# Strassen weight sums fetched two units ahead with other turns of the accumulators, and the mLSTM and SSD gates computed with tokens on the partitions

## The chip, the core and the metric

The kernel runs on one core of a Trainium2 chip. The metric is the device time of one execution in microseconds (us); each kernel is executed several times and the median counts. The engines named below are PE (matrix products; PEld is its weight load, which overlaps the products), DVE (vector), ACT (scalar), POOL (GpSimd) and SP, which issues DMAs. POOL and ACT issue DMAs as well. Each engine works through its own list of instructions in order.

## The reference

One layer of a streaming encoder in fp32 on 512 prompt tokens and 64 sample tokens, treated together as 576 columns. Cut to what matters here:

```python
h = x + 0.5 * swiglu(rmsnorm(x, norm_ffn1), w_ffn1_in, w_ffn1_out)     # 1024 -> 2*4096 -> 1024
h = h + mixer(rmsnorm(h, norm_mix))
h = h + 0.5 * swiglu(rmsnorm(h, norm_ffn2), w_ffn2_in, w_ffn2_out)
y = rmsnorm(h, final_norm)

def swiglu(x, w_in, w_out):
    a, b = split(x @ w_in, 2);  return (silu(a) * b) @ w_out

# mixer: one input projection feeds an SSD scan (16 heads), band attention (8 heads), an mLSTM (4 heads)
dt = softplus(dt_raw + ssd_dt_bias);  a = -exp(ssd_a_log)          # 16 heads
cum = cumsum(dt * a)                                               # within a chunk
ig = mi + gb[:4];  lf = log_sigmoid(mf + gb[4:])                   # 4 heads
b = cumsum(lf);  logd = b_t - b_s + ig_s;  m = running max(...)    # mLSTM gates and stabiliser
```

## The kernel before

**Products.** The three stages follow each other on one core: FFN 1 (0 to about 600 us of the span), the mixer (about 600 to 1410, its merge included) and FFN 2. Activations lie with features on partitions and the 576 tokens as columns. A product in fp32 is made of three matmuls of a faster type: each operand is split into a high and a low part (`split`, lines 271 to 274: a cast on ACT writes the tile `ph` of a weight or `TH` of an activation, a subtraction on DVE writes `pl` or `TL`), and high x high, high x low and low x high are added.

**Units.** Most of the work goes through `stream`, which multiplies by seven products instead of eight (Strassen's scheme in Winograd's form). A unit is a 1024 x 256 piece of a weight matrix, four blocks q0 to q3 of 512 x 128. Its seven weight operands are T_A11 = q0, T_A22 = q2, T_A21 = q3, and four sums: T_X1 = q0+q1, T_X2 = q1+q2, T_X3 = T_X1+q2, T_X4 = T_X3+q3. A product is 12 matmuls of 128 x 288. `fetch` loads the pair (q0, q1) into a tile of the ring `wx` with SP (line 444) and at once has POOL issue a DMA that adds (q1, q2) to it while it is being transferred (line 445); three more loads bring q0, q2, q3 into the ring `wr` (line 449). T_X3 and T_X4 are then added on POOL (line 455): in the FFNs in place, onto the tile of T_X1, so that the T_X3 sum waits until T_X1 has been split, and T_X4 until T_X3 has been.

**Order.** `stream` goes through the products by a list `order` in which products of unit n stand between those of unit n-1, has operands made AHEAD = 5 products before their use, and asks for the blocks of unit n and n+1 when it first makes an operand of unit n. Four of the seven products add into the accumulator of T_X1 (X1, X3, A22, X2, with a readout after each), two into that of T_X4 (X4, A21), and A11 has one by itself. In the FFNs each of the three has two PSUM banks, which alternate from unit to unit. The readouts are in `swiglu`: g (line 602, ACT), P (line 607, ACT), a (lines 610 and 614, DVE), and in `residual`: R (line 630, DVE). A scheduler that simulates the engines fixes the final order of instructions on each engine; what the program is written in is its starting point.

**Mixer.** Its heads run as generators (jobs) that are advanced by `tick` between the products. All of them share PSUM tiles of the tags `x` (one buffer), `v` (one) and `s` (two). The gates are a further generator, `gates`: 20 rows (16 SSD heads, 4 forget gates) lie on partitions 0 to 63 with the 576 tokens along the free axis, softplus is evaluated by a polynomial on DVE (lines 763 to 780), running sums and maxima by scans (lines 789, 794, 804), the rows are written to a scratch in DRAM (`scr_rows`) from which the heads load broadcast copies, and the whole is turned by five transposes into `TM`, with tokens on partitions (line 827).

Of the kernel before, what the change touches and what calls it, by code (L numbers as in the profile page):

```python
# [42 lines left out]
WBUFS = {"wr": 5, "wx": 3, "wy": 2, "ph": 6, "pl": 6}  # L43
# [16 lines left out]
C_AL = 133  # L60
C_M0 = 134
C_CS = 135
C_N = 183
# [15 lines left out]
class Hybrid:  # L79
    def __init__(self, ctx, tc, I, O):  # L80
        self.tc, self.nc, self.I, self.O = tc, tc.nc, I, O
        self.plan = []
# [58 lines left out]
    def hidden_tiles(self, name):  # L141

        self.hidden.close()
        self.hidden.enter_context(self.pools(name, yp=dict(side="right")))
        self.YH, self.YL = self.pair_of(self.yp, [128, 8, T], ("YH", "YL"))
# [36 lines left out]

    def sm(self):
        return self.small.tile([128, 8], F32, name="sm", tag="sm")

    def setup(self):
        nc, c = self.nc, self.const
        self.cst = c.tile([128, C_N], F32, name="cst")
        self.ones = c.tile([128, 128], F32, name="ones")
        nc.gpsimd.memset(self.ones, 1.0)  # L190
        self.mhalf = c.tile([128, 1], F32, name="mhalf")
        nc.gpsimd.memset(self.mhalf, -0.5)

        nc.scalar.activation(self.sm(), self.ones[:, 0:8], AF.Silu)
        warm = self.ps("x")
# [80 lines left out]
    def sumsq(self, x, k, h, acc, first=None):  # L276
# [5 lines left out]
        sq = self.small.tile([128, 320], F32, name="sq", tag="sq", bufs=2)  # L282
# [43 lines left out]
    def norm(self, x, g0, hi, lo):  # L326

        nc = self.nc
        with self.tc.high_priority(offset=1500):
            for h, (a, n) in enumerate(HALVES):  # L330
                sl = slice(a, a + n)
                acc = self.small.tile([128, 320], F32, name="na", tag="na", bufs=1)
# [7 lines left out]
    def norm_first(self, x, g0, hi, lo, pin):  # L340
# [4 lines left out]
        for h, (a, n) in enumerate(HALVES):  # L345
            sl = slice(a, a + n)
            sq = self.sqp.tile([128, 8, n], F32, name="sq0", tag=f"sq{h}")
# [16 lines left out]
    def norm_out(self, x, g0, out):  # L364

        nc = self.nc
        with self.tc.high_priority(offset=1500):
            for h in (1, 0):
                a, n = HALVES[h]
                sl = slice(a, a + n)  # L370
                acc = self.small.tile([128, 320], F32, name="na", tag="na", bufs=1)
                pt = self.ps("x")
                for k in range(8):
                    if h == 0 and k == 7:
                        sq = self.small.tile([128, 320], F32, name="sq", tag="sq", bufs=2)
# [60 lines left out]
    def fetch(self, desc):  # L436
# [8 lines left out]
        nc.gpsimd.dma_start(x12, src[:, 1:3, :], accum_op=ALU.add)  # L445
# [24 lines left out]
    def stream(self, seq, order, banks):  # L470
# [4 lines left out]
        raw, ops, st = {}, {}, {}  # L475
# [183 lines left out]
    def ffn(self, x, g0, win, wout, name, last=(0, 1)):  # L659
# [99 lines left out]
    def gates(self, pre):  # L759
        nc = self.nc  # L760
# [6 lines left out]
        nc.vector.reciprocal(d[S, :], d[S, :])
        nc.vector.tensor_tensor(d[S, :], u[S, :], d[S, :], op=ALU.mult)
        yield
        nc.vector.tensor_tensor(q[S, :], d[S, :], d[S, :], op=ALU.mult)  # L770
        nc.vector.tensor_scalar(p[S, :], q[S, :], 1.0 / 15, None, op0=ALU.mult)
        for m in (13, 11, 9, 7, 5, 3):
            nc.vector.scalar_tensor_tensor(p[S, :], p[S, :], 1.0 / m, q[S, :], op0=ALU.add, op1=ALU.mult)
            if m % 4 == 3:
                yield
        nc.vector.scalar_tensor_tensor(p[S, :], p[S, :], 1.0, d[S, :], op0=ALU.add, op1=ALU.mult)
        nc.vector.tensor_scalar(u[S, :], pre[S, :], 0.0, None, op0=ALU.max)
        yield
        nc.gpsimd.memset(RT[64:128, :], 0.0)
        nc.vector.scalar_tensor_tensor(RT[S, :], p[S, :], 2.0, u[S, :], op0=ALU.mult, op1=ALU.add)  # L780
        lf, b, g, M = u, d, p, q
        nc.vector.tensor_scalar(lf[0:4, :], RT[32:36, :], -1.0, None, op0=ALU.mult)
        yield
        na = self.small.tile([128, 8], F32, name="ga", tag="ga", bufs=1)
        self.tc.keep_in_program_order(nc.scalar.activation(na[0:16, 0:1], self.cst[0:16, C_AL:C_AL + 1], AF.Exp))
        nc.vector.tensor_scalar(na[0:16, 0:1], na[0:16, 0:1], -1.0, None, op0=ALU.mult)
        nc.vector.tensor_scalar(da[0:16, :], RT[0:16, :], na[0:16, 0:1], None, op0=ALU.mult)
        for a, n in CH:
            nc.vector.tensor_tensor_scan(RT[32:48, a:a + n], self.ones[0:16, :n], da[0:16, a:a + n], 0.0,
                                         op0=ALU.mult, op1=ALU.add)  # L790
        nc.sync.dma_start(self.scr[0:16, :], RT[32:48, :])
        yield
# [16 lines left out]
        nm, ei = lf, da  # L809
# [4 lines left out]
        nc.vector.tensor_scalar(nm[0:4, :], M[0:4, :], -1.0, None, op0=ALU.mult)  # L814
# [7 lines left out]
        nc.scalar.activation(RT[96:100, :], b[0:4, :], AF.Exp, scale=-1.0)  # L822
        for c, (a, n) in enumerate(CH):
            if c % 2 == 0:
                yield
            ps = self.ps("x")
            nc.tensor.transpose(ps[:n, 0:128], RT[:, a:a + n], self.ident)
            nc.vector.tensor_copy(self.TM[:n, c, :], ps[:n, 0:128])
# [530 lines left out]
    def run(self):  # L1359
        nc, tc = self.nc, self.tc  # L1360
        x = self.R1
        with self.ffn_phase("a"):
            xin = self.I["xT"].rearrange("(k p) t -> p k t", p=128)
            with self.pools("a0", sqp=None):
# [17 lines left out]
        with self.pools("m", acc=self.PS, psp=self.PS):  # L1382
# [3 lines left out]
            with self.pools("m", tp=None, gp=dict(side="right")):  # L1386
# [3 lines left out]
                nc.gpsimd.memset(self.TM[:, 4, :], 1.0)  # L1390
# [9 lines left out]
    def branches(self, x):  # L1400
# [3 lines left out]
        with self.pools("m0", xp=None, op=None):  # L1404
            self.XH, self.XL = self.pair_of(self.xp, [128, 8, T], ("XH", "XL"))
# [54 lines left out]
def pack(plans, inp):  # L1460
# [9 lines left out]
    gate[:, 32:36] = w["w_in"][:, O_MF:O_MF + 4]  # L1470
    gate[:, 64:68] = w["w_in"][:, O_MI:O_MI + 4]
# [64 lines left out]
```

## Time and profile before

| | us |
|---|---|
| median of 3 runs (1981.6 to 1982.52) | 1981.8 |
| profiled execution: its own time | 1983.52 |
| profiled execution: span of its instructions | 1981.8 |
| PE busy in it (96% of the span) | 1901.4 |
| PEld / DVE / ACT / POOL busy | 1824.5 / 1461.5 / 1083.3 / 673.0 |
| granted clock of PE, mean | 0.982 |

The span is the time from the first to the last instruction; 1.7 us of the execution lie around it. Busy time of PE includes the overlap of pipelined matmuls, so a PE that is busy throughout is not idle but not necessarily at its best rate; PEld, of which there is one load for each matmul, shows gaps a little earlier than PE. The times below are from the start of the span.

### The profile page before, as it was taken

The numbers are of one execution on the slowest core, as the hardware profiler recorded it, in microseconds if no ns is written. First come the engines' busy times: TensorE is split into PE (matmuls) and PEld (weight loads), VectorE is DVE, ScalarE is ACT, GpSimd is POOL, SyncE is SP. The second block draws the span as 40 slices with busy tenths as digits, with TensorE's granted clock in tenths as the row PEclk, the third lists the DMA queues.
The fourth block names the chain that finished last, engine by engine and source line by source line (L and its number), as shares of the span: only waits on it lengthen the run. The fifth ranks groups of instructions, "written<-read, shape, count | busy, mean of one in ns | idle before, by whom it ended". The sixth has DMA issues, their size and how long they took to land.

```text
span 1981.8 us, 37575 instructions
## 1 busy us (share of the span) xinstructions
PE 1901.4 (96%) x13889; PEld 1824.5 (92%) x13889; DVE 1461.5 (74%) x2727; ACT 1083.3 (55%) x2487; POOL 673.0 (34%) x662
## 2 busy tenths in 40 slices
PE   9999999999999889999989998899999999999998
PEld 8899999999999759978889897899999999999998
DVE  8987877877668958667676774665798787787765
ACT  4554554544545577677586874333555454454444
POOL 5343333333202215322443443351233333333311
PEclk9999999999999879999999998999999999999999
DMA  7267666666742535753656668652236666656631
GB/s 215 72 158 174 151 155 163 149 167 168 184 128 96 131 104 145 212 149 110 178 150 180 162 169 246 203 167 86 75 97 160 160 150 161 162 151 161 174 109 63
DMA packets 130079, 297.04 MB, mean 150 GB/s; under 512 B 14416, under 2 KB 26320, under 8 KB 129896
## 3 DMA queue, kind: packets, MB, share of 16 engines
q1 hardware_dynamic: 100648, 208.03, 33.0%
q0 software_dynamic: 19760, 72.10, 19.9%
q10 hardware_dynamic: 9488, 14.52, 2.4%
q8 instruction: 109, 1.79, 0.4%
q14 instruction: 74, 0.61, 0.1%
HBM read 274.04 MB, written 20.56 MB: 149 GB/s over the span
## 4 chain that ended last, share of the span: by engine, by line
PE 35%; DMA 8%; DVE 3%; ACT 3%; issue 2%; POOL 1%; ACTq 0%; DVEq 0%; POOLq 0%; SPq 0%
PE acc L591 21%; PE acc L244 12%; DMA wx<-in_sblk 6%; DMA R<-scr_rows 1%; DVE pl L273 1%; ACT ph L272 1%; DMA y<-ys 1%; ACT R L1188 1%; DVE TL L273 0%; PE ps_s L1206 0%; PE ps_v L1228 0%; PE ps_x L1235 0%; DVE P L639 0%; DVE g L639 0%; DMA ys<-g 0%
## 5 line engine op out<-in xcount | busy, mean ns | idle before, releaser
L591 PE MATMUL acc<-TH,ph 128*128 128x288 f32 x3220 | 959.0, 300 | 31.9 <-ACT g L602 10.4
L591 PE MATMUL acc<-TL,ph 128*128 128x288 f32 x3220 | 952.8, 297 | 0.1
L591 PE MATMUL acc<-TH,pl 128*128 128x288 f32 x3220 | 944.1, 297 | 6.6 <-DVE pl L273 6.1
L591 PEld LDWEIGHTS acc<-TH,ph 128*128 128x128 f32 x3220 | 605.6, 189 | 52.3 <-ACT g L602 13.4
L591 PEld LDWEIGHTS acc<-TH,pl 128*128 128x128 f32 x3220 | 604.6, 189 | 14.3 <-DVE pl L273 11.1
L591 PEld LDWEIGHTS acc<-TL,ph 128*128 128x128 f32 x3220 | 607.8, 189 | 2.5 <-issue 1.9
L273 DVE TENSOR_TENSOR pl<-wr,ph 128x512 fp32r<-128x512 f32 x471 | 404.2, 863 | 83.4 <-ACT ph L272 76.3
L272 ACT CAST ph<-wx 128x512 fp32r<-128x512 f32 x390 | 233.4, 619 | 334.4 <-POOL wx L455 154.3
L273 DVE TENSOR_TENSOR pl<-wx,ph 128x512 fp32r<-128x512 f32 x390 | 286.1, 745 | 169.0 <-ACT ph L272 165.2
L272 ACT CAST ph<-wr 128x512 fp32r<-128x512 f32 x471 | 286.1, 616 | 202.9 <-PE acc L244 99.9
L455 POOL TENSOR_TENSOR wx<-wx,wr 128x512 f32<-128x512 f32 x160 | 226.0, 1413 | 446.0 <-DVE pl L273 411.8
L244 PE MATMUL acc<-YH,ph 128*128 128x256 f32 (+1 forms) x768 | 227.1, 300 | 9.0 <-DVE y L1303 5.3
L244 PE MATMUL acc<-YL,ph 128*128 128x320 f32 (+1 forms) x768 | 228.8, 299 | 2.1 <-DVE YL L323 2.1
L244 PE MATMUL acc<-YH,pl 128*128 128x320 f32 (+1 forms) x768 | 226.8, 298 | 0.0
L445 POOL DMA_DIRECT2D wx<-in_sblk x115 | 101.6, 892 | 239.1 <-DMA wx<-in_sblk 84.1
L244 PEld LDWEIGHTS acc<-YH,ph 128*128 128x128 f32 x768 | 146.9, 193 | 10.4 <-DVE y L1303 5.5
L244 PEld LDWEIGHTS acc<-YL,ph 128*128 128x128 f32 x768 | 146.8, 192 | 3.2 <-DVE YL L323 2.6
L244 PEld LDWEIGHTS acc<-YH,pl 128*128 128x128 f32 x768 | 146.5, 192 | 0.0
L455 POOL TENSOR_TENSOR wy<-wx,wr 128x512 f32<-128x512 f32 x35 | 51.4, 1468 | 184.2 <-DMA wx<-in_sblk 73.6
L630 DVE SCALAR_TENSOR_TENSOR R<-acc,R 128x288 f32<-128x288 f32 x168 | 73.2, 449 | 0.6 <-PE acc L591 0.4
L272 ACT CAST TH<-g 128x288 fp32r<-128x288 f32 x120 | 51.2, 433 | 38.6 <-DVE g L639 19.7
L616 POOL TENSOR_TENSOR g<-g,P 128x288 f32<-128x288 f32 x56 | 56.6, 1010 | 43.9 <-ACT P L615 43.9
(296 smaller groups left out, 2414.5 us busy)
## 6 DMA issues: line engine op xcount, KB each, us to landing
wr<-in_sblk SPq DMA_DIRECT2D x345, 256.0 KB, 4.3
wx<-in_sblk SPq DMA_DIRECT2D x115, 512.0 KB, 3.9
wx<-in_sblk POOLq DMA_DIRECT2D x115, 512.0 KB, 7.0
wr<-in_wblk SPq DMA_DIRECT2D x126, 256.0 KB, 3.2
R<-scr_rows ACTq DMA_DIRECT2D x12, 576.0 KB, 5.8
gs<-g SPq DMA_DIRECT2D x24, 288.0 KB, 4.7
y<-gs POOLq DMA_DIRECT2D x24, 288.0 KB, 3.4
y<-ys POOLq DMA_DIRECT2D x16, 288.0 KB, 4.4
```

Source lines behind the costliest of these rows:

```text
L244: nc.tensor.matmul(ps[:, :n], wt[:, wsl], xx[:, k0 + k, a:a + n], start=(k == 0 and i == 0), stop=(k == nk - 1 and i == 2))
L272: self.nc.scalar.copy(hi, src)
L273: self.nc.vector.tensor_tensor(lo, src, hi.bitcast(F32), op=ALU.subtract)
L445: nc.gpsimd.dma_start(x12, src[:, 1:3, :], accum_op=ALU.add)
L455: add = lambda o, one, two: self.nc.gpsimd.tensor_tensor(o, one, two, op=ALU.add)
L591: self.nc.tensor.matmul(ps, wt[:, wsl], xx[:, kk, :], start=(start and kk == 0 and i == 0), stop=(kk == 3 and i == 2), skip_group_check=True)
L616: nc.gpsimd.tensor_tensor(s["g"][:, 1, :], s["g"][:, 1, :], a, op=ALU.mult)
L630: self.nc.vector.scalar_tensor_tensor(o, ps, scale, o, op0=ALU.mult, op1=ALU.add)
L1188: nc.scalar.activation(e[:n, a:a + n], e[:n, a:a + n], AF.Relu, scale=-1.0, bias=self.TM[:n, c, tc_:tc_ + 1])
```

## The change

1. **Fetching.** `fetch` is split. `fetch_sums` loads (q0, q1) two units ahead instead of one; POOL's adding DMA for unit n+2 is issued when T_X3 of unit n is made, thus no longer right behind the load. The loads of q0, q2, q3 stay one unit ahead. The ring `wx` has 4 tiles instead of 3; the room comes from the squares of the norms, which move from a pool that lives throughout into pools of the stages.
2. **Turns.** In the FFNs T_X2 of unit n-1 comes before T_X4 of unit n instead of after it, and the six PSUM banks are dealt as three for T_X1, one for A11, two for T_X4. The mixer's order and banks stay.
3. **Gates.** `gates` first transposes the 24 raw rows, so that tokens lie on partitions and 5 x 20 values along the free axis, evaluates softplus there, takes the cumulative sums with one product against the triangular mask, transposes back for the running maxima and writes `TM` directly. Its PSUM tiles are one of tag `x` four times, and one of tag `s` once.

The core of the diff:

```diff
-WBUFS = {"wr": 5, "wx": 3, "wy": 2, "ph": 6, "pl": 6}
+WBUFS = {"wr": 5, "wx": 4, "wy": 2, "ph": 6, "pl": 6}
...
-    def fetch(self, desc):
+    def fetch_sums(self, desc):
...
         x12 = self.ring("wx", shape=(128, 2, 512))
         nc.sync.dma_start(x12, src[:, 0:2, :])
-        nc.gpsimd.dma_start(x12, src[:, 1:3, :], accum_op=ALU.add)
-        raw = {"x12": x12}
+        return {"x12": x12, "src": src}, lambda: nc.gpsimd.dma_start(x12, src[:, 1:3, :], accum_op=ALU.add)
+
+    def fetch(self, raw):
         for q in (2, 3, 0) if self.mixer else (0, 2, 3):
             raw[q] = self.ring("wr")
-            nc.sync.dma_start(raw[q], src[:, q, :])
-        return raw
+            self.nc.sync.dma_start(raw[q], raw["src"][:, q, :])
...
         def make(n, t):
-            for m in (n, n + 1):
-                if m < len(seq) and m not in raw:
-                    raw[m] = self.fetch(seq[m][0])
+            for m in range(n, min(n + 3, len(seq))):
+                if m not in raw:
+                    raw[m], begin[m] = self.fetch_sums(seq[m][0])
+                if m in begin and (m < n + 2 or t == self.T_X3):
+                    begin.pop(m)()
+                if m < n + 2 and 0 not in raw[m]:
+                    self.fetch(raw[m])
             ops[n, t] = self.operand(raw[n], t)
...
-        order = ((0, self.T_X1), (1, self.T_A22), (0, self.T_A11), (1, self.T_A21), (0, self.T_X3), (0, self.T_X4),
-                 (1, self.T_X2))
-        self.stream(seq, order, lambda n: {t: 3 * (n % 2) + i for i, t in enumerate((self.T_X1, self.T_A11, self.T_X4))})
+        order = ((0, self.T_X1), (1, self.T_A22), (0, self.T_A11), (1, self.T_A21), (0, self.T_X3), (1, self.T_X2),
+                 (0, self.T_X4))
+        self.stream(seq, order, lambda n: {self.T_X1: n % 3, self.T_A11: 3, self.T_X4: 4 + n % 2})
...
     def gates(self, pre):
-        u, d, p, q, RT, da = (self.R1[:, i, :] for i in range(1, 7))
-        S = slice(0, 64)
-        nc.scalar.activation(u[S, :], pre[S, :], AF.Abs)
...
+        X, u, d, p, q = view(1, 24), view(2, 20), view(3, 20), view(4, 20), view(5, 20)
+        for c, (a, n) in enumerate(CH):
+            nc.tensor.transpose(ps[:n, c * 24:(c + 1) * 24], pre[0:24, a:a + n], self.ident[0:24, 0:24])
...
-            nc.vector.tensor_tensor_scan(RT[32:48, a:a + n], self.ones[0:16, :n], da[0:16, a:a + n], 0.0,
-                                         op0=ALU.mult, op1=ALU.add)
...
+        nc.tensor.matmul(ps[:, 0:100], self.mask, self.R1[:, 3, 0:100], start=True, stop=True)
+        nc.vector.tensor_copy(TM[:, :, 32:48], sums[:, :, 0:16])
...
+        for dst, r, m in ((b, 96, 4), (g, 64, 4), (RT, 32, 16)):
+            nc.scalar.copy(dst[0:m, 0:512], ps[r:r + m, :])
+            nc.scalar.copy(dst[0:m, 512:576], ps2[r:r + m, 0:64])
```

How it stands on the engines, at three places. First POOL in FFN 1, in a stretch of `swiglu` units; `wx<-in_sblk` is the adding DMA, `wx<-wx,wr` a T_X3 or T_X4 sum, `g<-g,P` a product of `swiglu`. Before:

```order
L445 DMA wx<-in_sblk 128x1024
L455 TENSOR_TENSOR wx<-wx,wr 128x512 x2
L616 TENSOR_TENSOR g<-g,P 128x288
L445 DMA wx<-in_sblk 128x1024
L455 TENSOR_TENSOR wx<-wx,wr 128x512 x2
```

and now:

```order
L451 DMA wx<-in_sblk 128x1024
L462 TENSOR_TENSOR wx<-wx,wr 128x512
L628 TENSOR_TENSOR g<-g,P 128x288
L462 TENSOR_TENSOR wx<-wx,wr 128x512
L451 DMA wx<-in_sblk 128x1024
```

The adding DMA stands between the two sums of a unit instead of ahead of or behind both, and serves the unit after next.

Second DVE at the start of the mixer's stream, where the gates begin; `R_60` is the tile that the gates work in, `pl` the low part of a weight, `g<-acc,uv` a readout of a product. Before:

```order
L767 RECIPROCAL R_60<-R_60 64x576
L273 TENSOR_TENSOR pl<-wy,ph 128x512
L273 TENSOR_TENSOR pl<-wx,ph 128x512
L517 SCALAR_TENSOR_TENSOR g<-acc,uv 128x288
L768 TENSOR_TENSOR R_60<-R_60 64x576
L517 SCALAR_TENSOR_TENSOR g<-acc,uv 128x288
```

and now:

```order
L279 TENSOR_TENSOR pl<-wr,ph 128x512
L791 RECIPROCAL R_60<-R_60 128x100
L529 SCALAR_TENSOR_TENSOR g<-acc,uv 128x288
L792 TENSOR_TENSOR R_60<-R_60 128x100
L529 SCALAR_TENSOR_TENSOR g<-acc,uv 128x288
L794 TENSOR_TENSOR R_60<-R_60 128x100
```

The same steps stand among the same neighbours, with 100 elements on a partition instead of 576.

Third PE later in the mixer, where for some time no product of `stream` (`acc`) stands in its list and two attention heads follow each other: `ps_x<-ident,P` turns probabilities, `ps_s<-g` makes scores, `ps_v<-Q,t` the weighted sums, `R_60` the gates' transposes, `ps_x<-ident,g` the next head's values. Before, from the last product on:

```order
L591 MATMUL acc<-TH_7247,pl 128x288
L827 MATMUL ps_x<-ident,R_60 128x128
L917 MATMUL ps_s<-g 128x384
L827 MATMUL ps_x<-ident,R_60 128x128
L903 MATMUL ps_x<-ident,P 128x128 x4
L903 MATMUL ps_x<-ident,P 64x128
L966 MATMUL ps_v<-Q,t 64x64 x8
L827 MATMUL ps_x<-ident,R_60 64x128
L966 MATMUL ps_v<-Q,t 64x64 x2
L917 MATMUL ps_s<-g 128x384
L858 MATMUL ps_x<-ident,g 128x128 x4
```

and now:

```order
L603 MATMUL acc<-TH_7252,pl 128x288
L931 MATMUL ps_x<-ident,P 128x128 x4
L983 MATMUL ps_v<-Q,t 64x128
L945 MATMUL ps_s<-g 128x256
L983 MATMUL ps_v<-Q,t 64x128 x7
L931 MATMUL ps_x<-ident,P 128x128 x4
L945 MATMUL ps_s<-g 128x384
L931 MATMUL ps_x<-ident,P 64x128
L994 MATMUL ps_v<-Q,t 64x64 x10
L886 MATMUL ps_x<-ident,g 128x128 x4
```

The gates' transposes have left this stretch, and the end of the first of the two heads has come into it: from the last product before it to the first behind it there are 58 instructions instead of 48. In the second half of the mixer's stream PE's list is the same in both kernels.

More of the change, by code (lines that the diff above doesn't have):

```diff
@@ L59 @@
 C_GB = 132
-C_AL = 133
+C_AL = 183
 C_M0 = 134
 C_CS = 135
-C_N = 183
+C_N = 203
 O_Z, O_X, O_B, O_C, O_DT = 0, 1024, 2048, 2560, 3072
@@ L143, in hidden_tiles @@
         self.hidden.close()
-        self.hidden.enter_context(self.pools(name, yp=dict(side="right")))
+        self.hidden.enter_context(self.pools(name, yp=dict(side="right"), qp=dict(side="right")))
+        self.sqp = self.qp, {"na": 1, "sq": 2}
         self.YH, self.YL = self.pair_of(self.yp, [128, 8, T], ("YH", "YL"))
@@ L181, in ps, with squares @@
         return self.psp.tile([128, 512], F32, name="ps_" + tag, tag=tag, bufs=self.pbufs[tag])
+    def squares(self, tag):
+        pool, bufs = self.sqp
+        if pool is self.op:
+            return self.op.tile([128, T], F32, name=bufs[tag], tag=bufs[tag], bufs=2)[:, :320]
+        return pool.tile([128, 320], F32, name=tag, tag=tag, bufs=bufs[tag])
     def sm(self):
@@ L281, in sumsq @@
             return
-        sq = self.small.tile([128, 320], F32, name="sq", tag="sq", bufs=2)
+        sq = self.squares("sq")
         nc.scalar.activation(sq[:, :n], x[:, k, a:a + n], AF.Square)
@@ L331, in norm @@
                 sl = slice(a, a + n)
-                acc = self.small.tile([128, 320], F32, name="na", tag="na", bufs=1)
+                acc = self.squares("na")
                 for k in range(8):
@@ L346, in norm_first @@
             sl = slice(a, a + n)
-            sq = self.sqp.tile([128, 8, n], F32, name="sq0", tag=f"sq{h}")
+            sq = self.s0.tile([128, 8, n], F32, name="sq0", tag=f"sq{h}")
             pt = self.ps("x")
@@ L370, in norm_out @@
                 sl = slice(a, a + n)
-                acc = self.small.tile([128, 320], F32, name="na", tag="na", bufs=1)
+                acc = self.squares("na")
                 pt = self.ps("x")
@@ L374, in norm_out @@
                     if h == 0 and k == 7:
-                        sq = self.small.tile([128, 320], F32, name="sq", tag="sq", bufs=2)
+                        sq = self.squares("sq")
                         nc.scalar.activation(sq[:, :n], x[:, k, sl], AF.Square)
@@ L771, in gates @@
-        nc.vector.tensor_scalar(p[S, :], q[S, :], 1.0 / 15, None, op0=ALU.mult)
-        for m in (13, 11, 9, 7, 5, 3):
[L773 to L777, printed above, removed]
-        yield
-        nc.gpsimd.memset(RT[64:128, :], 0.0)
@@ L796, in gates @@
-        nc.vector.tensor_copy(g[0:4, :], pre[64:68, :])
-        nc.vector.tensor_tensor(g[0:4, :], g[0:4, :], b[0:4, :], op=ALU.subtract)
-        nc.vector.tensor_copy(RT[64:68, :], g[0:4, :])
+        nc, TM = self.nc, self.TM
+        view = lambda i, w: self.R1[:, i, 0:5 * w].rearrange("p (c w) -> p c w", w=w)
+        X, u, d, p, q = view(1, 24), view(2, 20), view(3, 20), view(4, 20), view(5, 20)
+        nc.gpsimd.memset(X[64:128, 4, :], 0.0)
+        ps = self.ps("x")
+        for c, (a, n) in enumerate(CH):
+            nc.tensor.transpose(ps[:n, c * 24:(c + 1) * 24], pre[0:24, a:a + n], self.ident[0:24, 0:24])
@@ new lines, in gates @@
+        nc.vector.tensor_copy(X[:, 0:4, :], ps[:, 0:96].rearrange("p (c w) -> p c w", w=24))
+        nc.vector.tensor_copy(X[:64, 4, :], ps[:64, 96:120])
+        yield
+        S = X[:, :, 0:20]
+        nc.vector.tensor_scalar(X[:, :, 16:20], X[:, :, 16:20], -1.0, None, op0=ALU.mult)
+        nc.scalar.activation(u, S, AF.Abs)
+        nc.scalar.activation(u, u, AF.Exp, scale=-1.0)
+        nc.vector.tensor_scalar(d, u, 2.0, None, op0=ALU.add)
+        nc.vector.reciprocal(d, d)
+        nc.vector.tensor_tensor(d, u, d, op=ALU.mult)
@@ new lines, in gates @@
+        yield
+        nc.vector.tensor_tensor(q, d, d, op=ALU.mult)
+        nc.vector.tensor_scalar(p, q, 1.0 / 15, None, op0=ALU.mult)
+        for m in (13, 11, 9, 7, 5, 3):
+            nc.vector.scalar_tensor_tensor(p, p, 1.0 / m, q, op0=ALU.add, op1=ALU.mult)
+        nc.vector.scalar_tensor_tensor(p, p, 1.0, d, op0=ALU.add, op1=ALU.mult)
+        nc.vector.tensor_scalar(u, S, 0.0, None, op0=ALU.max)
+        sp = p
+        nc.vector.scalar_tensor_tensor(sp, p, 2.0, u, op0=ALU.mult, op1=ALU.add)
@@ new lines, in gates @@
+        na = self.R1[:, 5, 200:220]
+        self.tc.keep_in_program_order(nc.scalar.activation(na, self.cst[:, C_AL:C_AL + 20], AF.Exp))
+        da = d
+        nc.vector.scalar_tensor_tensor(da, sp, -1.0, na.unsqueeze(1).broadcast_to([128, 5, 20]),
+                                       op0=ALU.mult, op1=ALU.mult)
+        nc.vector.tensor_copy(TM[:, :, 0:16], sp[:, :, 0:16])
+        yield
+        ps = self.ps("x")
+        nc.tensor.matmul(ps[:, 0:100], self.mask, self.R1[:, 3, 0:100], start=True, stop=True)
@@ new lines, in gates @@
+        sums = ps[:, 0:100].rearrange("p (c w) -> p c w", w=20)
+        nc.vector.tensor_copy(TM[:, :, 32:48], sums[:, :, 0:16])
+        nc.vector.tensor_copy(TM[:, :, 96:100], sums[:, :, 16:20])
+        nc.vector.tensor_tensor(TM[:, :, 64:68], X[:, :, 20:24], TM[:, :, 96:100], op=ALU.subtract)
+        yield
+        RT, b, g, M, ei = (self.R1[:, i, :] for i in (6, 2, 3, 4, 5))
+        ps, ps2 = self.ps("x"), self.ps("s")
+        for c, (a, n) in enumerate(CH):
+            o = ps[:, a:a + n] if c < 4 else ps2[:, 0:n]
+            nc.tensor.transpose(o, TM[:n, c, :], self.ident[:n, :n])
@@ L813, in gates @@
         nc.sync.dma_start(self.scr[20:24, :], ei[0:4, :])
-        nc.vector.tensor_scalar(nm[0:4, :], M[0:4, :], -1.0, None, op0=ALU.mult)
+        nm = g
+        nc.scalar.activation(nm[0:4, :], M[0:4, :], AF.Copy, scale=-1.0)
         nc.sync.dma_start(self.scr[16:20, :], nm[0:4, :])
@@ L821, in gates @@
         nc.sync.dma_start(self.O["m"], mo[0:4, :])
-        nc.scalar.activation(RT[96:100, :], b[0:4, :], AF.Exp, scale=-1.0)
+        nc.scalar.activation(b[0:4, :], b[0:4, :], AF.Exp, scale=-1.0)
+        yield
+        ps = self.ps("x")
         for c, (a, n) in enumerate(CH):
[L824 to L828, printed above, removed]
+            nc.tensor.transpose(ps[:n, c * 4:c * 4 + 4], b[0:4, a:a + n], self.ident[0:4, 0:4])
+        nc.vector.tensor_copy(TM[:, 0:4, 96:100], ps[:, 0:16].rearrange("p (c w) -> p c w", w=4))
+        nc.vector.tensor_copy(TM[:64, 4, 96:100], ps[:64, 16:20])
     def rows(self, r0, n, step=0):
@@ L1363, in run @@
             xin = self.I["xT"].rearrange("(k p) t -> p k t", p=128)
-            with self.pools("a0", sqp=None):
+            with self.pools("a0", s0=None):
                 self.setup()
```

44 lines of the change are left out of this document (12 added, 32 removed).

## The prediction

> **What bounds the kernel now.** I read the page first, its line of engines:
>
> ```profile
> PE 1901.4 (96%) x13889; PEld 1824.5 (92%) x13889; DVE 1461.5 (74%) x2727; ACT 1083.3 (55%) x2487; POOL 673.0 (34%) x662
> ```
>
> PE is busy for 96%, so no more than the gaps of PE can be won unless its work shrinks, and the change removes none of it. Then I cut the span into stretches and looked for PEld's gaps, since there is one load for each matmul. Busy time of PE, PEld, DVE, ACT and POOL, the clock and the DMA share follow each other in these rows, two from the middle of each FFN's stream and one from near its end:
>
> ```profile
> 100.00:500.00 400.00, 390.89 (x2906) 386.24 (x2905) 307.66 (x544) 204.46 (x432) 147.41 (x128) 1.00 0.65 161
> 500.00:580.00 80.00, 80.00 (x611) 80.00 (x610) 53.16 (x100) 38.37 (x78) 12.36 (x12) 1.00 0.55 150
> 1490.00:1850.00 360.00, 350.79 (x2588) 344.40 (x2588) 276.61 (x488) 177.54 (x377) 130.32 (x113) 1.00 0.62 158
> 1850.00:1930.00 80.00, 80.00 (x604) 80.00 (x603) 56.85 (x89) 42.72 (x85) 22.13 (x20) 1.00 0.52 140
> ```
>
> Where nothing is late PEld is busy 80.00 of 80.00 us. In the two streams 400 - 386.24 = 13.8 and 360 - 344.40 = 15.6 us are missing: 29.4 us, all at full clock. That is what this change's first two parts can win. The waits of PEld name what ended them, FFN 1 first, then FFN 2 (us in total, times, longest):
>
> ```profile
> PEld acc L591 <- ACT g L602: 5.1, 4, 2.0
> PEld acc L591 <- DVE R L630: 4.1, 5, 1.2
> PEld acc L591 <- DVE pl L273: 2.4, 6, 1.0
> PEld acc L591 <- ACT P L607: 1.8, 4, 0.4
> ```
>
> ```profile
> PEld acc L591 <- ACT g L602: 8.0, 8, 2.2
> PEld acc L591 <- ACT P L607: 3.6, 7, 0.7
> PEld acc L591 <- DVE pl L273: 2.2, 9, 0.4
> PEld acc L591 <- DVE R L630: 0.9, 2, 0.5
> PEld acc L591 <- DVE g L618: 0.6, 1, 0.6
> ```
>
> PE is held by readouts of accumulators, not by weights. The timeline of ACT at one of the longest says why the readout was late; the last row is PE's:
>
> ```profile
> 376.98 0.62 ACT L272 CAST ph<-wx 128x512 fp32r<-128x512 f32 x1 [3.45 <-DMA wx<-in_sblk]
> 377.50 0.44 ACT L611 ACTIVATE P<-P 128x288 f32<-128x288 f32 x1
> 377.84 0.60 ACT L272 CAST ph<-wr 128x512 fp32r<-128x512 f32 x1
> 378.35 0.39 ACT L602 COPY g<-acc 128x288 f32<-128x288 f32 x1
> ```
>
> ```profile
> 378.79 0.40 PE L591 MATMUL acc<-TH,ph 128*128 128x288 f32 x1 [1.81 <-ACT g L602]
> ```
>
> ACT stood 3.45 us in front of a cast whose weight sum had not landed, and the copy that PE needed was three instructions behind it. Over the two streams ACT waits so often:
>
> ```profile
> ACT ph L272 <- DMA wx<-in_sblk: 47.4, 25, 3.7
> ```
>
> ```profile
> ACT ph L272 <- DMA wx<-in_sblk: 47.0, 24, 3.7
> ```
>
> Most of these waits are absorbed; those that are not are the g L602 and R L630 rows above.
>
> **The sums, two units ahead.** The path of a sum is SP's load, then POOL's adding DMA:
>
> ```profile
> wx<-in_sblk SPq DMA_DIRECT2D x115, 512.0 KB, 3.9
> wx<-in_sblk POOLq DMA_DIRECT2D x115, 512.0 KB, 7.0
> ```
>
> ```profile
> DMA to landing us min/median/max: 5.5/7.0/13.4
> ```
>
> ```profile
> 1850.00:1930.00 80.00, 68.01 (x509) 67.55 (x507) 1.00 0.52 140
> ```
>
> The first two rows are the load and the adding DMA from the page's list of issues, with their median time to landing; the third gives the spread of the adding one. The last row is line 591 alone: 68.01 / 509 = 0.134 us a matmul, so a product of 12 takes 1.60 us and a unit of 84 takes 11.2. Before, load and adding DMA need 3.9 + 7.0 = 10.9 us and are asked for one unit, 11.2 us, ahead of the cast: nothing is left for a queue, and the longest waits are 3.7 us. Now the load is asked for two units ahead (22.4 us). The adding DMA is issued four products later (6.4 us, over 3.9), so POOL no longer stands waiting for the load, and ten products, 16 us, before the cast, over the longest landing of 13.4. I take the g L602 and R L630 rows as gone: 5.1 + 4.1 + 8.0 + 0.9 = 18.1 us. Bytes and number of DMAs stay; the ring's fourth tile is released by the same unit n-2 as the third was, so SP's loads of q0, q2, q3, which stand behind the load of the pair, wait no longer than now.
>
> **The turns.** In the written order before, X1 of unit n+1 follows directly on X2 of unit n-1, which had its bank; the scheduler evades this by another order in which A22 comes closely behind X3, and P L607 is late. Now each readout has at least three other products, 4.8 us, before its accumulator is used again. Readouts take 0.39 us (row 378.35), so with a free queue this is enough: 1.8 + 3.6 + 0.6 = 6.0 us gone. The pl rows, 2.4 + 2.2 = 4.6 us, concern DVE's splitting and I let them stand. Sum of both parts: -24.1 us; bounds -29.4 (all gaps) and -12 (half, if DVE becomes late, below).
>
> **The gates.** Rows of DVE between 640 and 720 us (count, busy us, mean ns):
>
> ```profile
> L773 DVE SCALAR_TENSOR_TENSOR R<-R 64x576 f32<-64x576 f32 x6 | 5.0, 838 | 0.0
> L767 DVE RECIPROCAL R<-R 64x576 f32<-64x576 f32 x1 | 3.7, 3745 | 0.0
> L768 DVE TENSOR_TENSOR R<-R 64x576 f32<-64x576 f32 x1 | 1.5, 1477 | 0.0
> L780 DVE SCALAR_TENSOR_TENSOR R<-R 64x576 f32<-64x576 f32 x1 | 0.7, 741 | 0.0
> ...
> L1163 DVE TENSOR_TENSOR wd<-R,TM 128x4 f32<-128x4 f32 x2 | 0.3, 158 | 0.8 <-DMA R<-scr_rows 0.8
> ```
>
> From 4 to 576 elements an instruction grows from 158 to 741 ns, so 100 elements are an estimated 0.26 us (bounds 0.16 and 0.74) and the reciprocal 3.745 x 100/576 = 0.65. These four groups, 9 instructions and 10.9 us, become 8 x 0.26 + 0.65 = 2.7: DVE is relieved of 8 us there, and of some more by the scans that a product replaces. ACT gains six copies, three of them at most 0.6 us each. What it is worth stands in the stages and in PE's waits between 640 and 740 us:
>
> ```profile
> 640.00:710.00 70.00, 64.16 (x401) 53.77 (x399) 59.91 (x132) 43.96 (x109) 23.05 (x31) 0.93 0.55 151
> ...
> 709.00:734.50 25.50, 19.75 (x73) 9.09 (x72) 9.63 (x32) 15.64 (x52) 1.85 (x5) 0.60 0.29 66
> ```
>
> ```profile
> PEld acc L591 <- DVE g L517: 3.3, 2, 2.1
> ...
> PEld ps_x L903 <- ACT P L894: 3.5, 1, 3.5
> ```
>
> Up to 710 us DVE is busy 59.91 of 70 us, and PE's two groups of waits there, 6.8 us, hang on it; I take 5 of them as won. Against it stands the stretch without products behind it: 25.5 us at a clock of 0.60 for 48 of PE's instructions, 0.53 us each. There are 58 now, which costs 10 x 0.53 = 5.3 us. Together 0; bounds -9 (all waits won, the stretch unchanged, its clock better) and +8 (nothing won, three readouts later).
>
> **The rest of the mixer.** One stall there is of the kind above, ACT first, then PE:
>
> ```profile
> 952.69 0.62 ACT L272 CAST ph<-wx 128x512 fp32r<-128x512 f32 x1 [4.54 <-DMA wx<-in_sblk]
> ```
>
> ```profile
> 954.30 0.49 PE L1206 MATMUL ps_s<-t 128*128 128x128 f32 x2 [1.91 <-ACT st L1209]
> ```
>
> -1.9 us, bounds -4 and +4 since the order between 720 and 900 us shifts by a product or two.
>
> **The start.** One more adding DMA goes ahead of POOL's next work:
>
> ```profile
> 27.54 2.87 POOL L445 DMA_DIRECT2D wx<-in_sblk  x3
> 33.11 0.72 POOL L290 TENSOR_TENSOR sm<-sm,mhalf 128x2 f32<-128x2 f32 x1 [2.70 <-DVE sm L309]
> ```
>
> It takes about 1 us of the 2.70 that POOL waits anyway: 0; if that cover is gone, +1. The norms' squares have as many tiles as before: 0.
>
> **Sum.** -24.1 + 0 - 1.9 + 0 = -26.0 us. The profiled execution took 1983.5 us (span 1981.8 and 1.7 around it), the median of the runs shown is 1981.8, 0.1% less; 1957.5 for an execution like the profiled one, 1955.8 for the median. I forecast **1956 us**.
>
> **Rivals.** (A) DVE takes the place of ACT. PE then waits for pl and for readouts on DVE. For it: some splits of weights already run long in FFN 1 (x, min/median/max ns):
>
> ```profile
> L273 DVE TENSOR_TENSOR pl<-wx,ph x139: 673/685/1654, 99.4 to 499.6; 128x512 fp32r<-128x512 f32 x139
> L273 DVE TENSOR_TENSOR pl<-wr,ph x105: 673/684/1757, 101.7 to 494.8; 128x512 fp32r<-128x512 f32 x105
> ```
>
> The long ones lose 1.0 us each. If both POOL sums of each of the 36 units in that window cost DVE this much, that is at most 72 us on 307.66, 380 of 400: still under the window, but with no slack for bursts, and half the gain would go: 1981.8 - 12 = 1970. Against it: part of these losses is in the 307.66 already, and the number of sums does not change. The Trainium skill ("SBUF — State Buffer", section "Who interferes with whom") speaks for this rival: a vector instruction with two inputs in SBUF and a GpSimd instruction that reads SBUF shut each other out for a whole instruction. The maxima agree with it, and now X2's split stands between the two sums, where before DVE mostly waited. By the rule at its fullest the sum would be this rival's, by the medians mine.
>
> (B) The mixer wins too: with DVE free the first head ends earlier and the 25.5 us stretch shrinks by the 9 us above, with 3 to 4 more elsewhere: 1944. Against it: PE's list has more in that stretch, not less.
>
> (C) Slower. The new gates hold the only PSUM tile of tag x while ACT copies it six times, and the heads' turns wait for the same tile; the stretch without products grows. At 0.53 us an instruction it eats the 26 us from 49 more instructions, or from a length of 51.5 us, on; then 1986 and more. Against it: the list shows 10 more, not 49.
>
> (D) The change doesn't do what it says: sums land earlier, but ACT waits as long for POOL's sums (T_X3, T_X4) and PE for the same readouts: 1981.
>
> **Chances.** Forecast 0.62 (its own range 1946 to 1967), A 0.16, B 0.10, C 0.07, D 0.05. A change within 0.2%, 4 us, is about what a measurement of this kernel cannot tell from none. So faster 0.62 + 0.16 + 0.10 = 0.88, same 0.05, slower 0.07. The range takes in the forecast, most of B and of A: 1943 to 1974.
>
> **What would show it.** In the profile after, ACT's waits for the DMA of wx in the two windows fall from 94 us to below 10, PEld's gaps there from 29.4 to about 5, with pl as the first releaser; POOL's adding DMA waits for no load. DVE's busy time from 640 to 710 us falls by about 8; the stretch without products lasts about 31 us. Wrong would be: gaps of the old size under other names (A, D), or a stretch over 40 us at half clock (C).

## The result and the profile after

The changed kernel takes 1946.6 us (median of 4 runs, 1945.1 to 1949.5), the kernel before 1981.7: the ratio is 0.9825, its 95% interval 0.981 to 0.984. It is faster by 35 us; 26 were forecast. 1946.6 lies in the range, and nearer to rival B (1944) than to the forecast (1956). The profiled execution took 1949.5 us, its span is 1947.5. Its line of engines:

```profile
PE 1890.3 (97%) x13901; PEld 1824.7 (94%) x13901; DVE 1533.7 (79%) x2715; ACT 1099.2 (56%) x2494; POOL 669.9 (34%) x660
```

DVE is busy for 72 us more than before, although it has 12 instructions fewer and shorter gates. The stretches, with the columns of before (the last row is the new stretch without products in the mixer, now from 695.5 us on):

```profile
100.00:500.00 400.00, 397.72 (x2971) 395.82 (x2970) 361.26 (x551) 214.69 (x440) 151.42 (x132) 1.00 0.65 165
640.00:710.00 70.00, 65.22 (x406) 50.75 (x404) 43.62 (x122) 51.38 (x143) 17.04 (x21) 0.94 0.60 165
1490.00:1850.00 360.00, 357.94 (x2670) 355.59 (x2669) 317.85 (x492) 188.80 (x385) 135.83 (x117) 1.00 0.63 163
695.50:716.80 21.30, 20.07 (x90) 10.25 (x89) 8.82 (x27) 11.81 (x33) 1.92 (x4) 0.70 0.31 76
```

PEld's gaps in the two streams are 4.2 + 4.4 = 8.6 us instead of 29.4. What ended them, FFN 1 and then FFN 2:

```profile
PEld acc L603 <- ACT g L614: 2.3, 4, 0.9
PEld acc L603 <- DVE P L622: 1.5, 3, 0.5
PEld acc L603 <- ACT P L619: 0.3, 1, 0.3
```

```profile
PEld acc L603 <- ACT P L619: 1.7, 4, 0.5
PEld acc L603 <- DVE P L622: 1.7, 4, 0.5
PEld acc L603 <- ACT g L614: 1.0, 2, 0.5
```

ACT's waits for the DMA of `wx` (94 us in the two streams before) are gone; these are its two longest groups now, in FFN 1:

```profile
ACT ph L278 <- PE acc L603: 67.5, 84, 1.0
ACT ph L278 <- POOL wx L462: 52.8, 38, 3.4
```

The first means that ACT has its operands ready early and waits for PE to release a buffer, which is how it should be. For the stages I took the start of every matmul of 256, 288 or 320 columns on 128 x 128 weights; there are 12,684 in each kernel. The 4438th is one of the mixer's first products (at 629.8 us before), the 7608th stands in the mixer's merge, behind its heads (1267.1), so the rest is most of the merge and FFN 2. How much earlier than before the work got there in each profiled execution, as the gain of each stage in us (the kernel before took 1983.5 in its own):

| kernel | FFN 1 | mixer | rest | this execution, us | median us | ratio, 95% interval |
|---|---|---|---|---|---|---|
| the change | -10.6 | -13.5 | -10.2 | 1949.5 | 1946.6 | 0.981 to 0.984 |
| the change, run again | -9.9 | -19.3 | -8.2 | 1946.6 | 1949.8 | 0.982 to 0.986 |
| fetch alone | -14.9 | -2.0 | -16.8 | 1949.8 | 1957.3 | 0.985 to 0.990 |
| fetch alone, run again | -15.0 | -3.0 | -16.9 | 1948.6 | 1952.3 | 0.984 to 0.988 |
| turns alone | -11.5 | -3.3 | -12.8 | 1956.2 | 1956.8 | 0.986 to 0.990 |
| gates alone | -2.5 | -16.9 | -2.1 | 1962.6 | 1967.7 | 0.991 to 0.996 |
| fetch and turns | -11.8 | -3.9 | -11.8 | 1956.5 | 1959.1 | 0.987 to 0.991 |
| fetch and gates | -12.3 | -9.3 | -13.7 | 1948.2 | 1941.2 | 0.978 to 0.983 |
| turns and gates | -8.3 | -18.2 | -11.4 | 1945.6 | 1952.7 | 0.985 to 0.989 |

Ratios are to the kernel before on the same chip (its medians there were 1979.9 to 1982.5). A stage is that of one execution, which can lie off its kernel's median: fetch alone, gates alone, and turns and gates by 5 to 8 us below, fetch and gates by 7 above. The stages say three things that the sum of the forecast did not: each of the first two parts alone brings the gain in the FFNs, together they bring no more, and the gates bring most of the gain in the mixer.

### The profile page after: what moved, and what is told of

It reads as the page before. It is cut to its first block, busy times and chain, and to the rows that moved or that the text cites. A ratio compares the mean times of both kernels' runs of the same rounds, so it can differ in the third digit from the quotient of the medians.

```text
span 1947.5 us, 37732 instructions
## 1 busy us (share of the span) xinstructions
PE 1890.3 (97%) x13901; PEld 1824.7 (94%) x13901; DVE 1533.7 (79%) x2715; ACT 1099.2 (56%) x2494; POOL 669.9 (34%) x660
## 5 line engine op out<-in xcount | busy, mean ns | idle before, releaser
L279 DVE TENSOR_TENSOR pl<-wr,ph 128x512 fp32r<-128x512 f32 x471 | 445.2, 951 | 91.7 <-ACT ph L278 77.6
L279 DVE TENSOR_TENSOR pl<-wx,ph 128x512 fp32r<-128x512 f32 x390 | 323.2, 833 | 33.2 <-ACT ph L278 26.9
L462 POOL TENSOR_TENSOR wx<-wx,wr 128x512 f32<-128x512 f32 x160 | 245.9, 1537 | 191.5 <-DVE pl L279 154.1
L250 PE MATMUL acc<-YH,pl 128*128 128x256 f32 (+1 forms) x768 | 227.7, 298 | 0.0
L462 POOL TENSOR_TENSOR wy<-wy,wr 128x512 f32<-128x512 f32 x35 | 46.8, 1337 | 79.2 <-DVE pl L279 48.4
```

The lines of the kernel that those rows point to most:

```text
L250: nc.tensor.matmul(ps[:, :n], wt[:, wsl], xx[:, k0 + k, a:a + n], start=(k == 0 and i == 0), stop=(k == nk - 1 and i == 2))
L279: self.nc.vector.tensor_tensor(lo, src, hi.bitcast(F32), op=ALU.subtract)
L462: add = lambda o, one, two: self.nc.gpsimd.tensor_tensor(o, one, two, op=ALU.add)
```

## The experiments

**Each part by itself.** The kernel before with the lines of one part only (the diff's lines stand for the whole part):

```diff
-WBUFS = {"wr": 5, "wx": 3, "wy": 2, "ph": 6, "pl": 6}
+WBUFS = {"wr": 5, "wx": 4, "wy": 2, "ph": 6, "pl": 6}
...
-            for m in (n, n + 1):
+            for m in range(n, min(n + 3, len(seq))):
```

> Only the first part: sums loaded two units ahead, the adding DMA issued at T_X3, four tiles; turns and gates as before. Theory 1 (terms of the prediction): the waits that a late sum causes go, 18.1 us in the two FFN streams and 1.9 in the mixer: 1981.7 - 20 = 1962, and P L607's waits (5.4 us) stay. Theory 2: the 13.5 us that the changed kernel gained between 600 and 1245 us of its span are the work of the fetch, too: 1950 to 1955. Rival (DVE): splits that stand behind POOL's sums grow longer once DVE no longer waits, and half is lost: about 1971.

```diff
-        order = (... (0, self.T_X3), (0, self.T_X4), (1, self.T_X2))
+        order = (... (0, self.T_X3), (1, self.T_X2), (0, self.T_X4))
...
-        self.stream(seq, order, lambda n: {t: 3 * (n % 2) + i for i, t in enumerate((self.T_X1, self.T_A11, self.T_X4))})
+        self.stream(seq, order, lambda n: {self.T_X1: n % 3, self.T_A11: 3, self.T_X4: 4 + n % 2})
```

> Only the second part: T_X2 before T_X4 and banks dealt 3, 1, 2; fetch and gates as before. Theory 1: the waits on P L607 and g L618 go, 6.0 us: 1976. Rival: with sums one unit ahead the waits of ACT for the DMA of wx stay and the more regular order only renames the stalls: 1980 to 1983; if the fixed order takes away the scheduler's way to work around late sums, slower, up to 1990. The mixer's time does not change under any of them, since its order and banks are those of before.

```diff
-        u, d, p, q, RT, da = (self.R1[:, i, :] for i in range(1, 7))
+        X, u, d, p, q = view(1, 24), view(2, 20), view(3, 20), view(4, 20), view(5, 20)
```

> Only the third part: gates with tokens on partitions; fetch and turns as before. Theory 1 (the prediction): 0, between -9 and +8: 1981.7, with DVE's busy time between 640 and 710 us down by some 12 us. Theory 2 (from the trace of the changed kernel): the gates' relief of DVE is what shortened the mixer, -6.4 us up to its first attention heads and a part of the other 7.1 us by another order behind them: 1968 to 1975. Rival: nothing from the gates, the mixer gains only with the fetch: 1980 to 1983.

And the lines of the first two parts together:

> First and second part together, gates as before. Theory 1: -24.1 - 1.9: 1956. Theory 2 (gates shorten the mixer by 13.5 us): the FFNs' 21.5 us alone: 1960. Rival (the fetch shortens the mixer): 1947 to 1950, the time of the whole change. If the parts add, its gain is that of the first alone plus that of the second alone; if the turns are worth something only when sums are in time, it is more.

Fetch alone took 1957.3 us, its second run 1952.3. It took nearly all of PEld's gaps, 1.5 + 0.3 us are left, those of the turns' term (P, line 607) included:

```profile
100.00:500.00 400.00, 399.02 (x3003) 398.55 (x3003) 316.24 (x557) 215.91 (x445) 155.93 (x132) 1.00 0.65 166
1490.00:1850.00 360.00, 359.72 (x2710) 359.72 (x2711) 286.77 (x504) 192.05 (x395) 139.42 (x117) 1.00 0.65 166
```

Turns alone took 1956.8: 24 us gained on the same chip where 6 were expected, with sums asked for as late as before. Its gaps are 5.8 + 3.2 us:

```profile
100.00:500.00 400.00, 397.22 (x2966) 394.24 (x2966) 350.66 (x549) 212.77 (x439) 153.39 (x132) 1.00 0.64 165
1490.00:1850.00 360.00, 358.57 (x2686) 356.75 (x2685) 322.52 (x498) 190.62 (x389) 136.03 (x119) 1.00 0.64 165
```

How long a sum lies ready before its cast says much of why (24 units in FFN 1, from the landing of the adding DMA to the start of T_X1's cast, median): 0.1 us before, since the cast stood waiting; 1.2 with the turns; 9.8 with the fetch; 12.2 with both. The load came 12.0 us ahead of the cast before and with the turns alike. By the prediction's sum 10.9 us were needed and 11.2 were there: the sums were late by a hair, and with 1.1 us more slack ACT's waits for them are 10 us instead of 94 (the turns alone, FFN 1 and then FFN 2):

```profile
ACT ph L272 <- DMA wx<-in_sblk: 8.1, 6, 2.0
```

```profile
ACT ph L272 <- DMA wx<-in_sblk: 2.1, 2, 1.4
```

Beside the turns more slack was worth nothing: gaps of 9.0 us with 1.2, of 9.6 with 12.2. The two parts are two remedies for one wait, and their gains don't add. That in the turns alone the slack did it, and not the other deal of the banks, which came with it, is not shown.

Gates alone took 1967.7, just under the 1968 to 1975 of the theory by which they shorten the mixer. The first two parts together took 1959.1, as that theory had it, with gaps of 5.3 + 4.2 us: in the FFNs the pair is behind the fetch alone.

```profile
100.00:500.00 400.00, 397.25 (x2969) 394.65 (x2968) 357.49 (x551) 214.49 (x440) 152.15 (x131) 1.00 0.64 165
1490.00:1850.00 360.00, 358.37 (x2678) 355.78 (x2677) 323.88 (x498) 190.43 (x389) 135.98 (x118) 1.00 0.63 164
```

**Without the turns, without the fetch.** The change with the turns' lines taken back, and with the fetch's lines taken back:

> First and third part, turns as before: the change without its second part. In the first part's run alone 1.7 us of PEld's gaps were left in the two FFN stretches (1.5 + 0.2), with all three parts 8.6 (4.2 + 4.4), because DVE's splits behind POOL last longer. Theory 1: the turns cost these 7 us once sums are in time, so this kernel is 7 us faster than the whole change: 1939 to 1941. Theory 2: the parts add as medians, -23.5 - 13.2: 1945. Rival: the turns are needed by the whole and it is slower than the change, 1950.

> Second and third part, the sums fetched one unit ahead as before: the change without its first part. The turns alone moved the landing of a sum from 0.1 us before its cast, which stood waiting, to a median of 1.2 us. Theory 1: with the turns the fetch is worth nothing more, and PEld's gaps in the two FFN stretches stay at 8 to 10 us: within 4 us of the whole change, 1945 to 1951. Rival: 1.2 us is too little, some sums are late again and the fetch is worth 5 us and more beside the turns: 1954 or above.

> The changed kernel once more, for the comparison with the others on the same chip: 1946.5, between 1943 and 1950.

Fetch and gates took 1941.2, against 1949.8 for the change beside it; the intervals of the two ratios overlap a little, so the 8.6 us by themselves are not safe, but the stretches bear out a loss of that size: gaps of 0.5 and 0.0 us.

```profile
100.00:500.00 400.00, 399.91 (x3001) 399.46 (x3000) 313.32 (x555) 214.49 (x443) 154.61 (x131) 1.00 0.66 166
1490.00:1850.00 360.00, 360.00 (x2708) 360.00 (x2707) 285.73 (x500) 191.46 (x392) 139.25 (x117) 1.00 0.65 164
```

So the turns cost some 8 us in the FFNs once sums are in time (gaps of 8.6 against 0.5, and of 9.6 against 1.7 with the old gates). Turns and gates took 1952.7, with gaps of 6.1 + 3.1 us: between the two theories, and not to be told from the change.

**Where DVE's time goes.** The timeline of the change, POOL and then DVE at the same place, shows the price of the turns:

```profile
394.13 0.89 POOL L451 DMA_DIRECT2D wx<-in_sblk  x1 [4.66 <-DVE pl L279]
394.74 1.60 POOL L462 TENSOR_TENSOR wx<-wx,wr 128x512 f32<-128x512 f32 x1
395.99 1.10 POOL L628 TENSOR_TENSOR g<-g,P 128x288 f32<-128x288 f32 x1
```

```profile
394.31 3.34 DVE L279 TENSOR_TENSOR pl<-wr,ph 128x512 fp32r<-128x512 f32 x1 [0.42 <-ACT ph L278]
397.60 0.46 DVE L279 TENSOR_TENSOR TL<-g,TH 128x288 fp32r<-128x288 f32 x1
```

A split that takes 0.68 us alone lasts from 394.31 to 397.65, until POOL's sum and its product behind it are over. With the changed turns POOL does the DMA, a sum and the product in one go. The 248 splits of the stretch 100 to 500 by what POOL did meanwhile, their main groups (means worked out from the trace): 0.68 us beside nothing (164), 0.69 beside the DMA alone (12), 1.42 beside a sum (31), 2.31 beside a sum and the product (12), 3.17 beside all three (8). Splits over 2.2 us in both streams: 41 in the change's second run, 2 with fetch and gates. The profiled executions part the same way: the five with the turns in the table have 36 to 44 such splits and gaps of 8.6 to 9.6 us, the three with the fetch and without the turns 2 to 4 and 0.2 to 1.7. To test it, the product goes to DVE:

```diff
-                nc.gpsimd.tensor_tensor(s["g"][:, 1, :], s["g"][:, 1, :], a, op=ALU.mult)
+                nc.vector.tensor_tensor(s["g"][:, 1, :], s["g"][:, 1, :], a, op=ALU.mult)
```

> The changed kernel with one product of swiglu (line 628, g times P, 128x288) on DVE instead of POOL. Theory 1: DVE's splits wait out POOL's instructions that stand back to back. In the FFN 1 stretch 20 of them last 2.3 to 3.2 us because of such a product of POOL; without it DVE gets 24 x 0.45 = 10.8 us more work and is yet less busy, some 350 us of 400 instead of 361, and PEld's gaps in the two FFN stretches fall from 8.6 to 4 or less: 1942. Rival: no such waiting, DVE's busy time rises to 372, readouts on DVE come later and the gaps grow to 12 or more: 1950.

```profile
100.00:500.00 400.00, 398.65 (x2988) 397.94 (x2987) 359.41 (x581) 219.08 (x446) 133.43 (x108) 1.00 0.65 165
1490.00:1850.00 360.00, 360.00 (x2702) 360.00 (x2703) 325.06 (x516) 194.21 (x390) 116.76 (x96) 1.00 0.63 164
```

1939.9 us (ratio 0.978 to 0.982), gaps 2.1 + 0.0, splits over 2.2 us 15 instead of 41. In FFN 1 DVE does 30 instructions more in the window and is less busy (359.4, in the change 361.3 and 362.9); the fall to 350 did not come, and in FFN 2 it is busier, 325 instead of 318. So the gaps do not follow DVE's total; they follow the long splits, the longest of which is 2.6 us here instead of 3.4. The same edit on fetch and gates:

> First and third part, turns as before, and the product of line 628 on DVE: the two best kernels together. Theory 1: in the kernel without the turns only 2 splits in 480 last over 2.2 us and PEld's gaps in the FFN stretches are 0.5 us, so nothing is left that this could bring, and DVE, at 313 of 400 us, has room for 10.8 us more: 1941, within 4 us. Rival: the relief of POOL shortens the mixer, too, as the run with line 628 on DVE suggests (1940 with the turns in): 1933 to 1936.

1939.3 us (ratio 0.978 to 0.981), no gap at all in either window. Its interval lies below that of the change in both of its runs, so it beats the kernel before and the change; from the two kernels with 1941.2 and 1939.9 it is not to be told: nothing was left to win in the FFNs.

**What the gates are worth, and why.** In the change, DVE's eleven instructions of the polynomial get their old width back (`D`, `Pw`, `Q` are all 576 columns of the rows whose first 100 are `d`, `p`, `q`):

```diff
-        nc.vector.reciprocal(d, d)
+        nc.vector.reciprocal(D, D)
...
-            nc.vector.scalar_tensor_tensor(p, p, 1.0 / m, q, op0=ALU.add, op1=ALU.mult)
+            nc.vector.scalar_tensor_tensor(Pw, Pw, 1.0 / m, Q, op0=ALU.add, op1=ALU.mult)
```

> The changed kernel with the eleven DVE instructions of the gates' polynomial on 576 elements of each partition again, instead of 100 (the values in the other 476 are ones and not used); the rest of the gates as changed. By the rows of the kernel before these cost DVE some 10 us more. Theory 1: the mixer was shortened because DVE was relieved at its beginning: most of the 12 us that the gates brought are lost, 1955 to 1959, and a stretch without products of over 22 us with a half clock comes back. Rival: it was shortened because the gates' transposes left the stretch without products and the heads follow each other in another order: 1946 to 1949.

1962.1 us against 1949.8: the whole gain of the gates is lost, and a second stretch without products stands in the mixer, at 0.57 of the full clock. Its row, PE's longest wait there, and PE's timeline:

```profile
666.10:683.20 17.10, 14.02 (x30) 5.70 (x30) 11.10 (x33) 9.92 (x27) 0.87 (x1) 0.57 0.46 122
```

```profile
PEld ps_x L814 <- DVE R L808: 2.9, 1, 2.9
```

```profile
668.67 0.75 PE L814 MATMUL ps_x<-R,mask 128*128 128x100 f32 x2 [2.62 <-DVE R L808]
```

That fits the theory of DVE's time, but it has a second reading: the new gates have a product on PE (line 814 here, the cumulative sums) which stands in PE's list and waits for the polynomial. The other half of the test leaves that out: the old gates with a narrow polynomial, on fetch alone. Its kernel has no logarithmic term for most tokens, so it serves for its time alone:

```diff
-        nc.vector.reciprocal(d[S, :], d[S, :])
...
+        W = slice(0, 100)
...
+        nc.vector.reciprocal(d[S, W], d[S, W])
```

> First part alone with the gates of before, whose eleven DVE instructions of the polynomial work on 100 of the 576 elements of each partition; the logarithmic term of the other 476 tokens is left out (set to zero by POOL). DVE is relieved of about 9 us at the place where the new gates relieve it, and everything else of the old gates stays: scans, five transposes at the end, two copies less on ACT. Theory 1: DVE's time is what the gates' gain is made of: of the 16 us between the kernels with the first part and with the first and third (1957.3 and 1941.2), 10 or more come, 1942 to 1947. Rival: it is the other structure of the new gates (scans replaced by one product, the transposes earlier, the heads' order): 1953 to 1958.

> The first part alone once more, for the comparison on the same chip: 1957, between 1950 and 1961.

```profile
640.00:710.00 70.00, 59.23 (x369) 45.76 (x368) 44.90 (x124) 44.80 (x123) 17.73 (x20) 0.92 0.58 153
```

DVE is as free as in the change (44.9 of 70 us; 53.8 in fetch alone), and nothing is won: 1954.8 against 1952.3. So DVE's time by itself is not what the gain is made of, and the theory falls in that form; in the new gates the narrow polynomial is needed, as the run before shows, by DVE's time or by the product that waits for it. One thing that only the old gates have can be seen in both of these kernels. ACT's waits between 640 and 740 us in fetch alone (second run), and PE's longest beside them:

```profile
ACT Q L921 <- DMA scr_rows<-R: 3.2, 1, 3.2
ACT R L1211 <- DMA R<-scr_rows: 2.6, 2, 2.0
ACT el L1181 <- DMA R<-scr_rows: 2.4, 1, 2.4
```

```profile
PEld ps_x L918 <- ACT Q L921: 4.3, 5, 2.0
PEld ps_v L970 <- ACT Q L921: 3.9, 1, 3.9
```

ACT is about to issue the heads' loads from `scr_rows` and waits until the gates' sums, which come out of scans on DVE, have been written there; the copy that PE needs stands behind. The kernel with the narrow polynomial has the first wait too (2.5 us), the change has neither it nor PE's 3.9. In the kernel before and with the turns alone this one wait is not there, and the gates bring the mixer 17 and 15 us in them by the stages, so it is at most a part of the answer. By the medians the gates are worth 13 us by themselves and 11 to 18 beside the fetch, but only 4 beside the turns, whose execution with the gates in the table is the fastest of six.

One difference runs through all these kernels. The kernel before, the wide polynomial and the change's second run, from 620 to 740 us:

```profile
620.00:740.00 120.00, 108.68 (x665) 87.06 (x664) 91.44 (x209) 73.92 (x193) 30.92 (x41) 0.87 0.42 116
620.00:740.00 120.00, 109.13 (x677) 85.57 (x677) 87.61 (x199) 78.92 (x208) 32.62 (x44) 0.90 0.41 116
620.00:740.00 120.00, 113.20 (x798) 95.23 (x797) 92.17 (x220) 89.17 (x230) 37.52 (x47) 1.00 0.47 131
```

In the seven profiled executions with the old gates (narrow or not) or the wide polynomial PE is idle here for 10.6 to 15.7 us of the 120 and its granted clock is 0.87 to 0.90; in the seven with the new narrow gates it is idle for 6.8 to 7.2 us at a clock of 0.93 to 1.00. From the 4438th matmul of the count above to the 4953rd (629.8 to 760 us before) it takes 130 to 134 us in the first and 115 to 124 in the second, and that is where nearly all of the gates' gain in the mixer lies. So it goes with shorter pauses of PE and with a clock that falls less. The change's two runs show what the clock is worth in it: PE is idle for 6.8 us in both, and these matmuls took 123.8 us at 0.93 and 116.3 at 1.00. Whether the shorter pauses keep the clock up, and what in the new gates shortens them, no run here shows.

## Why the prediction was right, and where it was not

- *The total.* That it came out in the range is in part luck: in the profiled execution the FFNs brought 3.3 us less than the sum had, the mixer 11.6 more. Nor did all of it come out of PE's gaps: its busy time fell from 1901.4 to 1890.3 us with 12 instructions more, at a mean clock of 0.986 instead of 0.982.
- *The sums (-18.1) and the turns (-6.0).* Their total, -24.1, came out as -20.8 (10.6 + 10.2 by the stages), but the two terms were wrong. They were read from the names of what PE waited for: g and R to the fetch, P to the turns. The late sum was behind nearly all of them: fetch alone took 27.7 of the 29.4 us of gaps, P L607's included. The turns alone took 20.4, both together 20 to 21. (The fetch also moved POOL's adding DMA away from the load; no run tests that by itself.) The second term should have been zero or, beside the fetch, a loss of 8.
- *Rival A* took place in its cause and not in its price. It reckoned with at most 72 us for DVE, 380 of 400, and a gain cut to half, by 12 us. The splits beside POOL lost 84 x (1.54 - 0.68) = 72 us, DVE was busy for 361, and PE's gaps still fell to 8.6; the turns cost 8. The rule of the Trainium skill ("SBUF — State Buffer", section "Who interferes with whom"), that the one waits for a whole instruction of the other, agrees with the trace (1.42 us beside a sum, 0.68 alone); what I made of it for PE did not come. That the turns would bring it about I had seen as "X2's split between the two sums", and had not followed to POOL's list.
- *The gates (0).* This is the step that failed most: -9 to -19 us in the mixer in the seven profiled executions with the new narrow gates and +1 to -4 in those with the old or the wide ones; the bounds were -9 and +8. Alone the gates have a ratio of 0.991 to 0.996. The stretch without products was to grow by 10 instructions of 0.53 us. It has more of them (89 records of PEld instead of 72) and takes 21.3 us instead of 25.5. The 0.53 was not the price of an instruction: it held PE's waits for ACT and the low clock, and both shrank (a clock of 0.70 instead of 0.60, in the second run 1.00). DVE's relief at 640 to 710 us was 16 us, 13 in the second run, and not 8, but the run with the narrow polynomial shows that it alone brings nothing.
- *Rival B* (the mixer wins too, 1944) is what came in size: 13.5 and 19.3 us in the mixer, the stretch shorter by 4 and 10. Its reason, DVE free, is not borne out by the narrow polynomial.
- *The rest of the mixer (-1.9)* is not shown. The mixer gains 2 to 4 us with the fetch and the old gates, but 3.3 with the turns alone, too, which leave the mixer as it was; PE's wait at 954 us, 2.1 by its row for PEld, is gone with the fetch and only 0.4 with the turns alone. *The start (0)*: off by 2.3 us in the change, since the 634th matmul (at 108 us) came that much earlier; with the turns alone it was 2.9.
- *Signs.* ACT's waits on the DMA fell to nothing, as said. PEld's gaps were to be 5 with pl first; they are 8.6 with readouts first. That POOL's adding DMA waits for no load was wrong: it does so six times, for 23.6 us instead of 15.8 in the stretch of FFN 1, with 12 us of slack behind it.

```profile
POOL wx L451 <- DMA wx<-in_sblk: 23.6, 6, 5.9
```

Left open: which part of the gates' other structure, beside the late write to `scr_rows`, shortens PE's pauses and keeps the clock up; and why POOL's adding DMA waits for DVE (4.66 us in the row above) in the kernels with the turns and so comes to stand next to the sum.

## What to carry to other kernels

Waits that stand under several names in the list may have one cause; before their gains are added up, follow two of each back to what was late first, and ask of two remedies what the second is still worth when the first is in. Where a supply is late by a hair, a little slack can do what much slack does, as 1.2 us did here beside 12.2. A time per instruction taken from a stretch full of waits is no price for one more instruction there. Where PE pauses, look at the granted clock beside the waits.

## What the hardware showed that was not expected

DVE's subtraction of two SBUF tiles is held up not by one instruction of POOL only but by two that follow each other without a pause (0.68 us alone, 1.42 beside a sum, 2.31 beside a sum and a product), while the issue of POOL's DMA alone does not hold it up (0.69). And the same stretch without products (90 and 91 records of PE) took 21.3 us at a mean clock of 0.70 in one run of the change, above, and 15.7 in another where the clock stayed full:

```profile
694.30:710.00 15.70, 14.43 (x91) 7.58 (x89) 9.14 (x28) 11.91 (x36) 1.99 (x4) 1.00 0.42 106
```

These two runs of one kernel differ by 5.8 us in the mixer and by 2.7, the other way, in the other stages together.
